# The end of a norm in front of the first product chain that needs it, in a two-layer diffusion trunk

## The chip, the cores and the metric

The kernel runs on one core of one Trainium2 chip. The metric is the device time of one execution in microseconds (us); less is better. The engines that matter here are TensorE (PE, matrix products into PSUM), VectorE (DVE), ScalarE (ACT), GpSimd (POOL) and the queue that starts the weight loads (SP).

## What is computed

Two layers of one trunk over 512 latent tokens and 256 context tokens, width 1024. Cut to what matters:

```python
for layer in range(2):
    h  = h  + 0.5*g1 *swiglu(prenorm(h,  norm_ffn1, sh1, sc1),  ffn1_w_in, ffn1_w_out)
    hc = hc + 0.5*cg1*swiglu(prenorm(hc, norm_ffn1, csh1, csc1), ffn1_w_in, ffn1_w_out)
    zl = prenorm(h, norm_mix, shm, scm) @ w_in      # even or odd mixer
    zc = prenorm(hc, norm_mix, cshm, cscm) @ w_in
    ...                                             # Fourier + GLA, or short conv + differential attention
    h = h + gm*(mix_l @ mix_w_out)
    h = h + 0.5*g2*swiglu(prenorm(h, norm_ffn2, sh2, sc2), ffn2_w_in, ffn2_w_out)
    ...                                             # hc likewise, but not in the last layer
return rmsnorm(h, final_norm)

def prenorm(h, gain, shift, scale):
    return h * rsqrt(mean(h*h) + 1e-6) * gain * (1 + scale) + shift
```

## The kernel before

Activations lie transposed: 8 blocks of 128 features, with tokens along the free dimension (latent 0 to 512, context 512 to 768). Every float32 product is three products of split operands, (hi,hi), (lo,hi) and (hi,lo); a weight tile of 128 x 1024 is loaded by the SP queue, ACT rounds it to its high half `wh` (L170) and DVE subtracts to get its low half `wl` (L171). In the odd mixer `wl_engine` is GpSimd, so there the low half is made by POOL. Four buffers hold split weights; a fifth split waits until the oldest of the four is used up.

A norm is *deferred*. The products run on h times gain and scale (`ah`, `al`, made by `scale`, L613 and L614), and the factor R = rsqrt(mean + eps) is multiplied in afterwards, when a product is taken out of PSUM (`scaled`, L315). R is made in these steps. `norm_acc` squares each finished block on ACT (L535, L540) and adds the squares up on POOL (L544), block by block while the output products of the stage before end. Then `rstd` sums over the partitions with a matmul by ones (two instructions on PE, as `n<-R,ones` or, in the odd mixer, `mm<-R,ones`), ACT makes Identity, Ln and Exp of it (L560, L561, L564), and DVE makes R with three steps (L565, L566, L568). Ahead of them `done` preloads ACT's table set for Ln and Exp (L575).

`out_phase` ends a stage. For the half of the tokens that it finishes first it calls `done` itself; for the second half it stores `pending = [LATE, half, norm]`, LATE = 3, and the next stage ends the norm: `project`, which makes one chain of 8 x 3 products of one weight tile and one half, counts down and calls `norm_late()` ahead of the fourth chain, or, if its own half overlaps the pending half, calls `norm_late(hf)` behind its chain. That happens five times, each time for the second half: (a) from the first feed-forward block into the even mixer at about 590 us of the span, (b) from the even mixer into the next feed-forward block at 930, (c) into the third one at 1465, (d) from it into the odd mixer at 2000, and (e) from the odd mixer into the last feed-forward block at 2335. In (a), (b), (c) and (e) the first four chains belong to the other half (or, in (e), the first 256 latent tokens), so the count ends the norm ahead of the fourth. In (d) `head_proj(0)` makes, for the key weights, one context chain and then one latent chain of 512 columns, whose half is the pending one: there the norm is ended behind the second chain. The query chains (two of 256) and the value chains (context, latent) follow.

The order of the work: instructions are traced in program order and numbered, and the framework then plans one queue per engine with times of its own: whenever an engine is free in that plan, it takes, of the instructions that the plan holds ready, the one with the lowest number. `high_priority(offset=n)` lowers the numbers of the instructions in its block by n. `keep_in_program_order` ties an instruction behind the one traced before it on its engine: the table preload of `done` is tied so, and so are, in a `weave` (`pin`), the matmuls. On the chip each queue runs in the planned order and waits where the chip is later than the plan. `self.both` is False in the two mixers until their last filler, and True in the feed-forward blocks. HIP is 300. In the odd mixer three PSUM buffers (`ps0`) take the chains of `project`: the fourth chain needs the first one's buffer, the fifth the second one's.

Of the kernel before, what the change touches and what calls it, by code (L numbers as in the profile page):

```python
# [37 lines left out]
HIP = 300  # L38
# [80 lines left out]
class Net:  # L119
# [150 lines left out]
    def project(self, which, w, m, hf, c):  # L270


        if self.pending:
            self.pending[0] -= 1
            if self.pending[0] < 0:
                self.norm_late()
        t0, t1 = hf
        n = t1 - t0
        ps = self.mmt(which)[:m]
        w = tuple(x[:, :, :m] for x in w) if m < P else w  # L280
        a0 = self.acol(t0)
        if not self.defer or c is not None:
            yield from self.chain(ps[:, :n], w, self.A, a0, a0 + n)
            self.norm_late(hf)
            return ps[:, :n], c
        before = a0 == self.scol + 2
        a0 = min(a0, self.scol)
        yield from self.chain(ps[:, :n + 2], w, self.A, a0, a0 + n + 2)
        self.norm_late(hf)
        c = self.cpool.tile([P, 2], F32, tag="c", name=self.nm("c"), bufs=6)[:m]  # L290
        o = 0 if before else n
        with self.evac():
            self.nc.vector.tensor_copy(c, ps[:, o:o + 2])
        return ps[:, 2 * before:2 * before + n], c

    def norm_late(self, hf=None):

        if self.pending:
            _, late, last = self.pending
            if hf is None or hf[0] < late[1] and late[0] < hf[1]:  # L300
                self.pending = None
                last.done(late)

    def evac(self):

# [997 lines left out]
    def odd_mixer(self, halves, last):  # L1303
# [12 lines left out]
        with ExitStack() as es:  # L1316
# [42 lines left out]
            def head_proj(h):  # L1359
# [9 lines left out]
                def project(w, jobs, dst, rot=None):  # L1369
                    c = None  # L1370
                    for hf in jobs:
# [12 lines left out]
                        yield 0  # L1384

                yield from project(ws[0], (CT, LT), kr, kr[:, 0:SEQ])
                T = p2.tile([P, 2, TOK], F32R, tag="T", name=self.nm("T"))
                for s, (own, oth) in enumerate(((lo, up), (up, lo))):
# [3 lines left out]
                    nc.gpsimd.dma_start(B(T[oth, s, :]), kr[own, :])  # L1392
                ws.append(self.load_w(ow[18 + h], KD))
                yield from project(ws[1], (L1, L0), qr, qr)
                Q = [None, None]

# [8 lines left out]
                while h and (h - 1, 1) not in scored:  # L1405
                    yield None
                stack(0)
                vt = p1.tile([P, TOK], F32, tag="vt", name=self.nm("vt"))
                yield from project(ws[2], (CT, LT), vt)
                v = (p2.tile([P, TOK], F32R, tag="vh", name=self.nm("vh")),  # L1410
                     p2.tile([P, TOK], F32R, tag="vl", name=self.nm("vl")))
# [347 lines left out]
```

## Time and profile before

| what | value |
|---|---|
| time, median of 3 runs | 2729.46 us (2728.81 to 2730.92) |
| profiled execution, time | 2728.34 us |
| profiled execution, span | 2726.5 us |
| PE busy | 2662.0 us, 98% of the span |
| DVE, ACT, POOL busy | 1965.1, 1114.2, 305.6 us |
| mean granted TensorE clock | 0.992 |

The span runs from the first to the last instruction; the time has 1.8 us around it. A busy PE is a pipeline with matmuls in it and not PE at its peak.

### The profile page before, as it was taken

The numbers are of one execution on the slowest core, as the hardware profiler recorded it, in microseconds if no ns is written. First come the engines' busy times: TensorE is split into PE (matmuls) and PEld (weight loads), VectorE is DVE, ScalarE is ACT, GpSimd is POOL, SyncE is SP. The second block draws the span as 40 slices with busy tenths as digits, with TensorE's granted clock in tenths as the row PEclk, the third lists the DMA queues.
The fourth block names the chain that finished last, engine by engine and source line by source line (L and its number), as shares of the span: only waits on it lengthen the run. The fifth ranks groups of instructions, "written<-read, shape, count | busy, mean of one in ns | idle before, by whom it ended". The sixth has DMA issues, their size and how long they took to land.

```text
span 2726.5 us, 42007 instructions
## 1 busy us (share of the span) xinstructions
PE 2662.0 (98%) x16718; PEld 2441.8 (90%) x16718; DVE 1965.1 (72%) x3415; ACT 1114.2 (41%) x1852; POOL 305.6 (11%) x313
## 2 busy tenths in 40 slices
PE   9999999999999999999999999999999999999998
PEld 6888888888888879999998899999978888999998
DVE  6699999777889876655666766656678887755545
ACT  4312121255545643323436534333456566523323
POOL 2000000030000200100002100000142323100002
PEclk9999999999999999999999999999999999999999
DMA  7466665622111034434422444334222222342332
GB/s 264 136 206 192 194 205 184 228 72 86 55 51 63 28 97 113 110 83 112 112 75 61 105 108 111 89 96 119 78 86 63 68 56 72 119 142 79 97 97 63
DMA packets 114276, 298.24 MB, mean 109 GB/s; under 512 B 13136, under 2 KB 22704, under 8 KB 114080
## 3 DMA queue, kind: packets, MB, share of 16 engines
q1 hardware_dynamic: 98448, 264.52, 30.4%
q0 software_dynamic: 14544, 29.99, 6.1%
q8 instruction: 132, 2.16, 0.3%
q10 hardware_dynamic: 1088, 1.05, 0.1%
q14 instruction: 64, 0.52, 0.1%
HBM read 285.55 MB, written 2.10 MB: 105 GB/s over the span
## 4 chain that ended last, share of the span: by engine, by line
PE 82%; DVE 12%; ACT 3%; issue 2%; DMA 1%; SPq 0%; POOL 0%; DVEq 0%; ACTq 0%; POOLq 0%
PE mm L176 80%; DVE al L614 1%; DVE hlat L639 1%; DVE mx L1444 1%; DVE gS L1245 1%; PE sc L176 1%; DVE wl L171 1%; ACT wh L170 1%; ACT e L1446 1%; PE n L176 1%; PE mm L183 0%; DVE atl L152 0%; DVE hctx L639 0%; DVE ry L1354 0%; DVE e L1458 0%
## 5 line engine op out<-in xcount | busy, mean ns | idle before, releaser
L176 PE MATMUL mm<-ah,wh 128*128 128x258 f32 (+3 forms) x2896 | 947.3, 327 | 7.5 <-DVE t L315 4.0
L176 PE MATMUL mm<-ah,wl 128*128 128x258 f32 (+3 forms) x2896 | 930.8, 322 | 3.4 <-DVE wl L171 3.4
L176 PE MATMUL mm<-al,wh 128*128 128x258 f32 (+3 forms) x2896 | 932.3, 322 | 0.0
L170 ACT ACTIVATE wh<-wr 128x1024 fp32r<-128x1024 f32 (+2 forms) x393 | 377.4, 960 | 798.4 <-PE mm L176 627.9
L176 PEld LDWEIGHTS mm<-ah,wh 128*128 128x128 f32 x2896 | 548.6, 189 | 43.5 <-DVE t L315 4.8
L176 PEld LDWEIGHTS mm<-ah,wl 128*128 128x128 f32 x2896 | 547.9, 189 | 34.6 <-DVE wl L171 5.0
L176 PEld LDWEIGHTS mm<-al,wh 128*128 128x128 f32 x2896 | 548.8, 190 | 27.5 <-issue 1.7
L176 PE MATMUL mm<-hh,wh 128*128 128x256 f32 (+1 forms) x1408 | 459.5, 328 | 9.2 <-DVE hctx L639 5.4
L176 PE MATMUL mm<-hh,wl 128*128 128x256 f32 (+1 forms) x1408 | 458.8, 327 | 2.1 <-DVE wl L171 2.1
L176 PE MATMUL mm<-hl,wh 128*128 128x256 f32 (+1 forms) x1408 | 459.4, 327 | 0.0
L171 DVE TENSOR_TENSOR wl<-wr,wh 128x1024 fp32r<-128x1024 f32 (+2 forms) x357 | 395.4, 1109 | 48.2 <-ACT wh L170 47.6
L176 PEld LDWEIGHTS mm<-hh,wh 128*128 128x128 f32 x1408 | 267.0, 190 | 38.0 <-DVE hctx L639 8.3
L176 PEld LDWEIGHTS mm<-hh,wl 128*128 128x128 f32 x1408 | 267.4, 190 | 26.6 <-DVE wl L171 2.7
L176 PEld LDWEIGHTS mm<-hl,wh 128*128 128x128 f32 x1408 | 267.6, 190 | 23.3
L639 DVE SCALAR_TENSOR_TENSOR hlat<-mm,mod,hlat 128x512 f32<-128x512 f32 (+1 forms) x248 | 163.1, 661 | 167.7 <-PE mm L176 167.1
L492 DVE SCALAR_TENSOR_TENSOR junk<-ada,cond 128x1024 bf16<-128x1024 f32 x224 | 273.0, 1219 | 3.4 <-DMA ada<-in_adaT_dram 3.0
L315 DVE TENSOR_TENSOR t<-mm,R 128x256 f32<-128x256 f32 (+1 forms) x216 | 106.5, 494 | 103.5 <-PE mm L176 103.0
L785 POOL DMA_DIRECT2D sg<-in_ffn_in_dram x80 | 71.0, 1015 | 849.5 <-DVE hctx L639 356.1
L151 ACT ACTIVATE hh<-t 128x256 fp32r<-128x256 f32 (+2 forms) x136 | 79.6, 585 | 174.2 <-DVE t L716 151.0
L544 POOL TENSOR_TENSOR nacc<-nacc,nsq 128x256 f32<-128x256 f32 x47 | 37.6, 800 | 969.8 <-ACT nsq L540 929.9
L858 DVE SCALAR_TENSOR_TENSOR t<-mm,R 128x386 f32<-128x386 f32 x40 | 22.4, 560 | 126.7 <-PE mm L176 126.7
L714 ACT ACTIVATE t<-t,c 128x256 f32<-128x256 f32 (+1 forms) x96 | 54.1, 563 | 136.5 <-DVE t L315 133.5
(317 smaller groups left out, 3657.7 us busy)
## 6 DMA issues: line engine op xcount, KB each, us to landing
wr<-in_ffn_in_dram SPq DMA_DIRECT2D x136, 512.0 KB, 3.4
ada<-in_adaT_dram SPq DMA_DIRECT2D x128, 512.0 KB, 3.8
wr<-in_ffn_out_dram SPq DMA_DIRECT2D x48, 512.0 KB, 4.1
sg<-in_ffn_in_dram SPq DMA_DIRECT2D x80, 256.0 KB, 3.1
sg<-in_ffn_in_dram POOLq DMA_DIRECT2D x80, 256.0 KB, 5.5
wr<-in_ffn_out_dram SPq DMA_DIRECT2D x48, 384.0 KB, 3.3
wr<-in_odd_w_dram SPq DMA_DIRECT2D x24, 512.0 KB, 3.3
wr<-in_even_w_dram SPq DMA_DIRECT2D x21, 512.0 KB, 3.3
```

What stands on the lines that cost most here:

```text
L151: self.nc.scalar.activation(hi, src, AF.Copy)
L170: self.nc.scalar.activation(hi, rv, AF.Copy)
L171: self.wl_engine.tensor_tensor(lo, rv, hi.bitcast(F32), op=ALU.subtract)
L176: i = self.nc.tensor.matmul(*a, **k)
L315: self.nc.vector.tensor_tensor(dst, ps, self.R[:ps.shape[0], hf[0]:hf[1]], op=ALU.mult)
L492: nc.vector.scalar_tensor_tensor(junk, w, 1.0, self.cond[:, s, :], op0=ALU.mult, op1=ALU.mult, accum_out=self.mods[l][:, s, n:n + 1]))
L544: self.acc_engine.tensor_tensor(acc[:, :w], acc[:, :w], sq[:, :w], op=ALU.add)
L614: nc.vector.scalar_tensor_tensor(lo[:, a], self.hv(k, s0, s1), G, hi[:, a].bitcast(F32), op0=ALU.mult, op1=ALU.subtract)
L639: nc.vector.scalar_tensor_tensor(hv, ps[:, s0 - t0:s1 - t0], gate, hv, op0=ALU.mult, op1=ALU.add)
L714: nc.scalar.activation(sg, sg, AF.Silu, bias=c[0][:, st:st + 1])
L785: nc.gpsimd.dma_start(out, y, accum_op=ALU.add)
L1245: nc.vector.scalar_tensor_tensor(S[r, c1, :], S[r, c0, :], EL[r, c0:c0 + 1], U[c0][r], op0=ALU.mult, op1=ALU.add)
```

## The change

Two edits. In `project`, where the count has not run out and `both` is False, a pending norm whose half overlaps the chain's own is ended in front of the chain and not behind it. And `norm_late` traces the end of the norm under a priority that is 300 numbers higher.

```diff
@@ -274,6 +274,8 @@
             self.pending[0] -= 1
             if self.pending[0] < 0:
                 self.norm_late()
+            elif not self.both:
+                self.norm_late(hf)
         t0, t1 = hf
         n = t1 - t0
         ps = self.mmt(which)[:m]
@@ -299,7 +301,8 @@
             _, late, last = self.pending
             if hf is None or hf[0] < late[1] and late[0] < hf[1]:
                 self.pending = None
-                last.done(late)
+                with self.tc.high_priority(offset=HIP):
+                    last.done(late)
```

## Rows read from the trace of the kernel before

**Rows 1.** Page, part 1: busy us (share of the span) xinstructions
```profile
PE 2662.0 (98%) x16718; PEld 2441.8 (90%) x16718; DVE 1965.1 (72%) x3415; ACT 1114.2 (41%) x1852; POOL 305.6 (11%) x313
```

**Rows 2.** Waits, PE: waiting for, us in total, times, longest
```profile
PE mm L176 <- DVE t L315: 4.0, 1, 4.0
```

**Rows 3.** Timeline, PE at (d): start, us, operation [idle before <- releaser]
```profile
1994.70 0.28 PE L176 MATMUL mm<-ah,wh 128*128 128x258 f32 x1
...
1997.60 0.39 PE L176 MATMUL mm<-ah,wh 128*128 128x512 f32 x1
...
2003.69 1.13 PE L176 MATMUL mm<-R,ones 128*128 128x512 f32 x2 [0.37 <-POOL R L544]
...
2010.25 0.28 PE L176 MATMUL mm<-ah,wl 128*128 128x256 f32 x1
2014.58 0.39 PE L176 MATMUL mm<-ah,wh 128*128 128x258 f32 x1 [4.04 <-DVE t L315]
```

**Rows 4.** Timeline, ACT at (d), behind the ones matmul
```profile
2006.48 0.51 ACT L1381 ACTIVATE kr<-kr,c 128x256 f32<-128x256 f32 x1 [4.86 <-DVE kr L315]
2007.00 1.28 ACT L575 ACT_TABLE_LOAD   x1
2008.30 1.06 ACT L170 ACTIVATE wh<-wr 128x1024 fp32r<-128x1024 f32 x1
2009.26 0.67 ACT L560 ACTIVATE R<-mm,eps 128x512 f32<-128x512 f32 x1
```

**Rows 5.** Timeline, DVE at (d)
```profile
2001.70 4.27 DVE L1348 SCALAR_TENSOR_TENSOR nlam<-lam 128x1 f32<-128x1 f32 x1
...
2011.20 1.14 DVE L565 TENSOR_TENSOR R<-R,t 128x512 f32<-128x512 f32 x1 [4.76 <-ACT t L564]
2012.38 0.69 DVE L566 SCALAR_TENSOR_TENSOR R<-R,t 128x512 f32<-128x512 f32 x1
...
2013.83 0.69 DVE L315 TENSOR_TENSOR t<-mm,R 128x512 f32<-128x512 f32 x1
```

**Rows 6.** Timeline, POOL at (d)
```profile
2002.35 1.29 POOL L544 TENSOR_TENSOR R<-R,nsq 128x512 f32<-128x512 f32 x1
2003.59 2.36 POOL L171 TENSOR_TENSOR wl<-wr,wh 128x1024 fp32r<-128x1024 f32 x1
2009.44 2.36 POOL L171 TENSOR_TENSOR wl<-wr,wh 128x1024 fp32r<-128x1024 f32 x1 [3.49 <-ACT wh L170]
```

**Rows 7.** Windows, PE alone: stretch, us, busy (instructions), granted clock, DMA
```profile
2015.04:2018.36 3.32, 3.32 (x18) 0.52 0.00 0
```

**Rows 8.** Timeline, ACT at (d), ahead of the ones matmul
```profile
1998.07 0.73 ACT L613 ACTIVATE ah<-hlat,mod 128x512 fp32r<-128x512 f32 x1 [2.84 <-DVE hlat L639]
...
1999.22 1.04 ACT L170 ACTIVATE wh<-wr 128x1024 fp32r<-128x1024 f32 x1
```

**Rows 9.** Timeline, PE and POOL at (b)
```profile
932.13 1.36 POOL L544 TENSOR_TENSOR R<-R,nsq 128x512 f32<-128x512 f32 x1 [0.74 <-ACT nsq L540]
935.57 6.72 POOL L544 TENSOR_TENSOR R<-R,nsq 128x512 f32<-128x512 f32 x3 [2.09 <-ACT nsq L540]
...
938.03 0.36 PE L176 MATMUL mm<-ah,wh 128*128 128x258 f32 x1 [0.71 <-DVE hlat L639]
...
943.95 1.02 PE L176 MATMUL n<-R,ones 128*128 128x512 f32 x2
```

**Rows 10.** Timeline, POOL and PE at (a)
```profile
597.58 1.30 POOL L544 TENSOR_TENSOR R<-R,nsq 128x512 f32<-128x512 f32 x1
...
602.40 1.02 PE L176 MATMUL n<-R,ones 128*128 128x512 f32 x2
```

**Rows 11.** Timeline, POOL at (c)
```profile
1468.57 1.32 POOL L544 TENSOR_TENSOR R<-R,nsq 128x512 f32<-128x512 f32 x1 [0.90 <-ACT nsq L540]
```

**Rows 12.** Timeline, POOL and PE at (e)
```profile
2332.95 3.28 POOL L544 TENSOR_TENSOR R<-R,nsq 128x256 f32<-128x256 f32 x3 [0.88 <-ACT nsq L540]
...
2335.69 0.39 PE L176 MATMUL mm<-ah,wl 128*128 128x258 f32 x1 [1.29 <-DVE wl L171]
```

## The prediction

> **What bounds the kernel now.** I read the page first, then the waits of PE, then the timelines of the four engines at the five places where a pending norm is ended. The page says that PE is busy for 98% of the span [rows 1]. So whatever this change does, it does by taking idle time of PE away or adding some. The waits of PE name one that belongs to a pending norm: a single wait of 4.0 us for the product that is multiplied by R [rows 2]. It lies at (d), the head of the odd mixer; at (a), (b), (c) and (e) no PE wait is put down to R.
>
> At (d) the reader is to see this. The context key chain starts at 1994.70, the latent one at 1997.60, the ones matmul follows it at 2003.69 after 0.37 us of waiting for POOL's last add, the query chains run until 2010.54, and the context chain of the values starts only at 2014.58, because the PSUM buffer of the latent key chain is not yet free [rows 3]. Behind the ones matmul ACT is held back: by an activation that comes after a late DVE step, then a table load of 1.28, then a weight split of 1.06 from 2008.30; only then comes the first step of R, at 2009.26 [rows 4]. DVE's three steps follow at 2011.20, the first of them slow at 1.14, and the product is read at 2013.83 [rows 5]. The wait has a second price: at 2015.04 to 2018.36 PE runs at a granted clock of 0.52, that is the lower of its two levels (1.2 GHz of 2.4 GHz), after it had stood idle for 4.04 us [rows 3, 7]. Sixteen product intervals lie in that stretch of 3.32 us. At the upper level one takes 0.121 (the 24 products of the context key chain fill 1994.70 to 1997.60 [rows 3]), so sixteen would take 1.94, and the stretch costs about 1.4 us.
>
> **The change, part by part.** Nothing is added or removed: the same two ones matmuls, three activations, one table load and three DVE steps are issued, no DMA is moved, and SP is passed by nothing. What changes is where they stand in four queues.
>
> First edit. It acts at (d) alone: in the even mixer the first four chains belong to the other half, so there the count still ends the norm, and the feed-forward blocks have `both` True. At (d) the ones matmul moves in front of the latent key chain in program order. The table load stays tied behind the same activation, since the chain that it is moved past has no ACT instruction.
>
> Second edit. All five ends get a number lower by 300. Three chains with their evacuations are some 100 numbers, so the ones matmul now beats all of the chains around it wherever the plan holds it ready, at all five places. That is the point on which I cost the change: PE's queue runs in order, and the ones matmul will stand where the *plan* expects POOL's last add, while the chip may be later. Queued behind it are the products of the running chain, which need nothing of R.
>
> How far is the plan ahead of the chip? At (d) the ACT queue tells it. The split at 1999.22 writes buffers that came free with the last output product, which on the chip came just ahead of 1994.70 [rows 3], and it stands behind the activation that the chip starts at 1998.07 after 2.84 us of idleness [rows 8]. Had the plan seen that idleness it would have filled it with the split; so in the plan that activation starts by 1994.7, at least 3.4 us ahead of the chip.
>
> At (d), then: R's last add ends on the chip at 2002.35 + 1.29 = 2003.64 [rows 6], and in the plan some 3.4 to 5 us earlier in the chip's reckoning, that is at 1998.6 to 2000.2, inside the latent key chain. PE will stop there until about 2003.7, for 3.5 to 5.1 us; I take the middle, 4.3. The bounds are today's 0.37 and 6.1 (a stop at the chain's very start, 2003.69 - 1997.60). After it PE has no reason to stop later: today's work ends at 2010.54 with 0.37 of waiting in it, so the value chain starts at 2010.54 - 0.37 + 4.3 = 2014.5 where it now starts at 2014.58. R's own path: ACT's split of 1.06 gives way [rows 4], and DVE's first step loses its stretch of 1.14 - 0.69 = 0.45 if POOL's half of that split no longer runs beside it [rows 5, 6], so the buffer is free 1.5 us earlier, at 2013.1, and no longer decides. The stall of 4.04 goes and one of 4.3 takes its place in front, with the same low clock behind it. Net: 0.0, between -1.5 -1.4 = -2.9 (no early stop, and the clock holds) and +1.7 (a stop of 6.1).
>
> At (b): the ones matmul stands at 943.95 today, but R is ready at 935.57 + 6.72 = 942.29 [rows 9]. The three adds take 6.72, while the one before took 1.36 and three of these 4.08: the chip may be 2.64 later than a plan in which nothing disturbs them, and the 0.71 that PE waits for the last block's update there is a second lateness of the same sort. Cost of a stop between 0 and 3.35; no row says which end, so I take the half, 1.7. PE has no later wait there that would swallow it.
>
> At (a) R is ready at 597.58 + 1.30 = 598.88, well ahead of today's ones matmul at 602.40 [rows 10]; (c) is of the same form, with its last add at 1468.57 [rows 11]. The adds are undisturbed, so the lateness should be no more than one of them: 0 to 1.3 each, and I take 0.65 each. At (e) R is ready at 2332.95 + 3.28 = 2336.23, and PE waits for a split until 2335.69 in any case [rows 12]: 0 to 0.54, taken as 0.3. Nothing is gained at these four: today R is there before the first latent evacuation asks for it or holds no one up, since no PE wait names it [rows 2].
>
> Precedence on ACT and DVE costs nothing: weight splits that give way by one or two steps have been made ahead of need everywhere but at (e), where PE already waits 1.29 for one [rows 12], and the norm's steps there come behind that split.
>
> Sum: 0.0 + 1.7 + 0.65 + 0.65 + 0.3 = +3.3. Against the profiled execution 2728.34 + 3.3 = 2731.6; the median of the runs shown is 1.1 above that execution, so the forecast is 2732.8 us.
>
> **A rule that speaks against the gain at (d).** While POOL's split half runs from 2003.59 for 2.36 us, a DVE step on one column per partition lasts from 2001.70 to 2005.97, and the first step of R lasts 1.14 where the next takes 0.69 while the next split half runs [rows 5, 6]. If the split gives way on ACT by the norm's three activations it starts at about 2010.1, and its POOL half at 2011.2, just on DVE's third step: that would hold until 2013.6, and the buffer would be free at about 2014.9, later than now. The Trainium skill, page "SBUF — State Buffer", section "SBUF: two separate sides", says of the port pair of VectorE and GpSimd that it is an exclusive lock, held for the whole instruction, and that the loser fully blocks. By that rule the trace agrees.
>
> **The rivals.** *It does what it says* (faster, but little): the plan is near the chip, so no queue stops early, and the wait at (d) shrinks by 1.5, from 4.04 to 2.5, with or without the low clock behind it: -1.5 to -2.9, middle -2.0, time 2727.5. For it speaks that today's ones matmul waits for POOL only 0.37 [rows 3]; against it the place of the split in ACT's queue [rows 8]. *The collision above*: no early stop, but DVE's third step held by POOL: +0.4, time 2729.9. *The stops are at their upper ends* (slower): if PE stops at (b) for 3.35, at (a) and (c) for 1.3, at (e) for 0.54 and at (d) for 6.1, that is 3.35 + 2.6 + 0.54 + 1.7 = 8.2, and a stop of over 3 us at (b) may bring the low clock's 1.4: +9.6, time 2739.1. It decides from the point where the plan puts POOL's last add ahead of the chip by more than 2 us at (b). *The whole wait at (d) goes*: 4.04 + 1.4 = 5.4, time 2724.1. Against it: the table load stays tied behind an activation that ends at 2007.0, so R cannot be there before about 2012.
>
> **How the numbers follow.** Forecast 0.48, it does what it says 0.25, collision 0.07, upper ends 0.15, whole wait 0.05. A measurement of this kernel tells about 0.2% from no change, 5.5 us: 2724.0 to 2734.9. Faster by more takes the whole wait or a reordering further on in the odd mixer: 0.06. Slower takes the upper ends and the upper part of the forecast, whose own range is 2729.5 to 2736: 0.21. The rest, 0.73, is within 0.2%. The range of 8 in 10 reaches from 2726.0 (the second case with nearly all of its 2.9) to 2737.5.
>
> **What would show it.** Right: the ones matmul at (d) stands inside the latent key chain with a PE wait of 3 to 5 us for POOL L544, and the wait for DVE t L315 is gone or under 1 us; at (b) the ones matmul stands ahead of 943 with a PE wait of 1 to 3 us for POOL L544; ACT's split follows the norm's activations at (d). Wrong: no PE wait names POOL L544 beyond today's, or the ones matmuls of (a), (b) and (c) stand where they stood; then the second case holds. A third step of DVE of 2 us at (d) would show the collision.

## The result, and the profile after

The changed kernel takes 2745.80 us (median of 6 runs, 2744.99 to 2746.51) against 2729.52 us (6 runs, 2728.81 to 2730.92): a ratio of 1.0059 with a 95% interval of 1.0046 to 1.0072, 16.3 us slower. The forecast was 2732.8 us, with a range that ended at 2737.5. The sign of the sum was right and its size a fifth of what came. The profiled execution takes 2744.99 us with a span of 2742.9.

Part 1 of the page shows that PE does the same work in a longer span [rows 1]: its busy time is 0.5 us longer, the span 16.4.

```profile
PE 2662.5 (97%) x16718; PEld 2440.6 (89%) x16718; DVE 1967.0 (72%) x3415; ACT 1113.8 (41%) x1851; POOL 305.5 (11%) x313
```

The waits of PE name what is new (waiting for, us in total, times, longest):

```profile
PE n L176 <- POOL R L547: 10.5, 4, 3.9
PE mm L176 <- DVE hctx L642: 6.9, 6, 1.5
PE mm L176 <- DVE hlat L642: 5.9, 9, 1.1
PE mm L176 <- POOL R L547: 5.4, 1, 5.4
PE mm L176 <- DVE wl L171: 4.2, 6, 1.2
PE sc L176 <- DMA Q<-Q: 2.0, 2, 1.5
```

Five waits for POOL's last add, 15.9 us in all, stand where the kernel before had one of 0.37 [rows 3]; the wait of 4.0 for `t` [rows 2] is gone. The waits for `hctx` and `hlat` (the hidden states after an update) grew by 1.5 and 1.0 (5.4 and 4.9 before), that for `wl` shrank by 1.4 (5.6 before), that for the query's transfer grew by 1.5 (0.5 before). The timeline of PE shows the five ends in order (start, us, operation, idle before and its releaser):

```profile
599.85 1.13 PE L176 MATMUL n<-R,ones 128*128 128x512 f32 x2 [2.29 <-POOL R L547]
...
945.81 2.07 PE L176 MATMUL n<-R,ones 128*128 128x512 f32 x2 [3.90 <-POOL R L547]
...
1480.24 1.12 PE L176 MATMUL n<-R,ones 128*128 128x512 f32 x2 [1.80 <-POOL R L547]
...
2016.87 2.07 PE L176 MATMUL mm<-R,ones 128*128 128x512 f32 x2 [5.43 <-POOL R L547]
...
2351.51 0.70 PE L176 MATMUL n<-R,ones 128*128 128x256 f32 x2 [2.50 <-POOL R L547]
```

At each end PE stands still at the ones matmul until R's last add is there: 2.29 at (a), 3.90 at (b), 1.80 at (c), 5.43 at (d), 2.50 at (e). At (b) and (d) the two instructions also last 2.07 us, where they took 1.02 and 1.13 before [rows 3, 9]: they run at the lower clock. The windows of PE alone show how long that holds (stretch, us, busy and instructions, granted clock, then DMA):

```profile
601.00:605.00 4.00, 4.00 (x35) 1.00 0.09 21
945.80:950.70 4.90, 4.89 (x17) 0.50 0.39 108
1482.00:1486.00 4.00, 4.00 (x35) 1.00 0.01 4
2016.80:2022.60 5.80, 5.74 (x12) 0.50 0.48 166
2353.00:2357.00 4.00, 4.00 (x36) 1.00 0.70 206
```

Behind the stops of (a), (c) and (e) the granted clock is 1.00; behind those of (b) and (d) it is 0.50 for 4.9 and 5.8 us, PE's level of 1.2 GHz. What this costs: at (b) the ones matmuls and 14 products run from 945.81 to 950.69, 4.88 us; at the upper level the ones take 0.56, the first product behind them 0.52 and thirteen more 0.121 each, 2.65; so 2.2. At (d) the ones and ten products of 512 columns take 5.98, from 2016.87 to 2022.85; at the upper level 0.56 + 0.64 + 9 x 0.231 = 3.28 (the 0.64 is the first such product behind the ones in the run call_wlv below); so 2.7.

Where the time came from, stage by stage: I take the starts of the ones matmuls of the *first* halves, which the change doesn't move, as marks, each named after the end that follows it (the table is worked out from their rows in the two timelines of PE).

| from mark to mark | before, us | after, us | difference |
|---|---|---|---|
| (a) to (b) | 338.35 | 340.90 | +2.55 |
| (b) to (c) | 533.17 | 539.99 | +6.82 |
| (c) to (d) | 529.52 | 532.42 | +2.90 |
| (d) to (e) | 341.19 | 343.19 | +2.00 |
| (e) to the last norm | 380.72 | 381.92 | +1.20 |

The start up to (a) is 0.95 longer; there the waits for the first weight transfers differ, and the mark lies between 579.1 and 581.6 in the kernels of this document, most of which leave that stretch as it was. The stops and the clock account for most of the rest: (a) 2.29; (b) 3.90 + 2.2, which leaves 0.7; (c) 1.80, which leaves 1.1; (d) 5.43 - 0.37 for POOL, less the 4.04 for `t`, less the 1.4 of low clock behind that [rows 3, 7], plus 2.7, which makes 2.3; at the first scores, where PE now waits 1.5 for the query's transfer and before 0.6 for `kr`, it is 2.8, and 2.0 at the next mark; (e) 2.50, less the wait of 1.29 for `wl` [rows 12], which the stop covers.

How far to trust the small remainders: in seven kernels that leave everything from (b) to (c) as it was that stretch takes 533.17 to 533.82 us, before being the shortest, so the 0.7 is hardly more than this scatter. In eight that leave (c) to (d) as it was it takes 529.52 to 529.89, so the 1.1 is more, and it came again in the run not_d; its cause is open. It is not the longer waits for `hctx` and `hlat`, 1.0 and 1.4 us more, 40 to 55 us behind the stops of (b) and (c): the run call_only has the same waits at (b), and hip25 at (c), without a stop there. The clock scatters too. From a ones matmul ahead of (e) (`mm<-osq,ones`, at 2293.88 before) to the mark of (e) the kernel before takes 27.59 us, with the granted clock at 0.50 for 6.7 us of them, the changed one 26.58 with 3.4, and head_late, a run below, 24.99 with none. So 1.0 came back there, and up to that matmul the changed kernel is 3.0 behind. The edits don't decide it: not_d and b_only both leave the odd mixer as it was and have 3.3 and 6.6 us of it.

At (d) ACT did what the change is for (timeline of ACT):

```profile
2019.63 0.51 ACT L1384 ACTIVATE kr<-kr,c 128x256 f32<-128x256 f32 x1 [4.79 <-DVE kr L318]
2020.14 1.28 ACT L578 ACT_TABLE_LOAD   x1
2021.43 0.69 ACT L563 ACTIVATE R<-mm,eps 128x512 f32<-128x512 f32 x1
2022.02 0.68 ACT L564 ACTIVATE t<-mm,eps 128x512 f32<-128x512 f32 x1
2022.73 0.63 ACT L567 ACTIVATE t<-t 128x512 f32<-128x512 f32 x1
2025.60 1.06 ACT L170 ACTIVATE wh<-wr 128x1024 fp32r<-128x1024 f32 x1 [2.24 <-PE mm L176]
```

The norm's three activations follow the table load at once, and the split comes 2.24 us behind them; before, it stood in front of them [rows 4]. R is no longer late, but PE had by then lost 5.43 us.

### The profile page after: what moved, and what is told of

It reads as the page before. It is cut to its first block, busy times and chain, and to the rows that moved or that the text cites. A ratio compares the mean times of both kernels' runs of the same rounds, so it can differ in the third digit from the quotient of the medians.

```text
span 2742.9 us, 42006 instructions
## 1 busy us (share of the span) xinstructions
PE 2662.5 (97%) x16718; PEld 2440.6 (89%) x16718; DVE 1967.0 (72%) x3415; ACT 1113.8 (41%) x1851; POOL 305.5 (11%) x313
```

## The experiments

Two theories to begin with. *The plan's lead*: each end's ones matmul now stands in PE's queue where the plan holds R ready; the chip is later, and PE stops for the difference. *Precedence*: splits that give way on ACT and DVE, or the moved call, make the loss. A first answer is in the plans: a variant that raises the ones matmul alone, and leaves ACT's and DVE's steps their numbers, is planned into the same five queues as the whole change; one that raises only those steps, at the old calls, is planned into before's queues, with at most one table load of ACT in another place. So in the plan the priority acts through the ones matmul. By the places in PE's queue it stands 49, 47, 49 and 51 instructions ahead of its old place at (a), (b), (c) and (e), and 22 at (d).

**One edit alone** (call_only). The first edit without the priority:

```diff
-                with self.tc.high_priority(offset=HIP):
-                    last.done(late)
+                last.done(late)
```

> The first edit alone: the norm's end in front of the chain, no priority. On PE only the ones matmul of (d) moves, by 22 places, into the latent key chain as with the whole change; those of (a), (b), (c) and (e) stand as before. Theory 1 (the loss is made at each end where the ones matmul stands ahead of POOL's last add, and is the stop there plus the low clock behind it): only (d) pays, +2.0 us, 2731.5 us, with one PE wait of about 5.4 us for POOL at (d) and none at the other ends. Rival (the moved call makes the loss): about 2745 us. Rival (the change gains at (d)): below 2729 us.

It measured 2730.93 us, ratio 1.0006 (0.9997 to 1.0015), 1.3 us more. PE's timeline at (d):

```profile
2004.32 2.07 PE L176 MATMUL mm<-R,ones 128*128 128x512 f32 x2 [5.43 <-POOL R L546]
```

The stop is the one of the whole change, with no other wait for POOL; the marks give +1.57 from (d) to (e). The time's interval includes no difference; that the stop is there, and that nothing moved elsewhere, is read from the rows.

**The other four places alone** (not_d). The priority at (a), (b), (c) and (e), (d) as before:

```diff
-            elif not self.both:
-                self.norm_late(hf)
...
+                self.ends += 1
-                with self.tc.high_priority(offset=HIP):
+                with self.tc.high_priority(offset=HIP if self.ends in (1, 2, 3, 5) else 0):
```

> The priority at (a), (b), (c) and (e), with (d) ended behind the latent key chain and without priority, as before. Theory 1: the whole change less the 2.0 us of (d): +14.3, 2743.8 us, four PE waits for POOL as with the whole change, and the wait of 4.0 us for t at (d) is back. Rival (the odd mixer's head makes the loss): about 2731 us.

It measured 2742.77 us, ratio 1.0048 (1.0035 to 1.006), +13.2. The waits of PE:

```profile
PE n L177 <- POOL R L547: 10.5, 4, 3.9
PE mm L177 <- DVE t L318: 4.0, 1, 4.0
```

The four stops and the old wait at (d) are there as expected. This run and the one before add up to +14.5 of the 16.3. In its profile the clock also fell behind the stop of (a), where it had held in the whole change; the last section comes back to that.

**One place alone** (b_only). The same for (b) alone:

```diff
-                with self.tc.high_priority(offset=HIP if self.ends in (1, 2, 3, 5) else 0):
+                with self.tc.high_priority(offset=HIP if self.ends in (2,) else 0):
```

> The priority at (b) alone, without the first edit. Theory 1: a stop of 3.9 us for POOL at (b), the clock at 0.50 for some 5 us behind it (2.2 us), and 0.5 to 1 us more at the next stage's start: +6.1 to +7.1, 2735.7 to 2736.7 us, and nothing at the other ends. Rival (the stop alone costs, the clock is hidden): +3.9, 2733.5 us.

It measured 2736.64 us, ratio 1.0027 (1.0016 to 1.0037), +6.5: the stop and the clock behind it.

```profile
942.98 2.07 PE L177 MATMUL n<-R,ones 128*128 128x512 f32 x2 [3.91 <-POOL R L547]
...
944.00:949.00 5.00, 5.00 (x25) 0.58 0.21 59
949.00:955.00 6.00, 6.00 (x52) 1.00 0.00 0
```

The first line is of the timeline, the others are windows as above: granted clock 0.58 in the first 5 us, 1.00 behind. By the marks (b) to (c) is 6.98 longer, so the rival, the stop of 3.9 alone, falls.

**The dose** (hip35 and hip25). The whole change with 35 and with 25 in place of 300. The ones matmul of (b) then stands 17 and 24 products later than with 300.

```diff
-                with self.tc.high_priority(offset=HIP):
+                with self.tc.high_priority(offset=35):
```

> The whole change with an offset of 35 numbers in place of 300. The ones matmuls of (a), (b), (c), (e) then stand 30 products ahead of their old place and not 47 to 51, so 19, 17, 19 and 21 products later than with 300; (d) as with 300. Theory 1: a product is 0.121 us, so the stops shrink by 2.3, 2.1, 2.3 and 2.5 us: from 2.29, 3.90, 1.80 and 2.50 to 0, 1.8, 0 and 0, and after a stop of 1.8 us the clock stays at 1.00. Sum 1.8 to 2.8 at (b) and 2.0 at (d): 2733.3 to 2734.3 us. Rival (precedence over the splits on ACT and DVE makes the loss; any priority does it): about 2745 us.

> The whole change with an offset of 25. The ones matmul of (b) stands 7 products later than with 35 and 24 later than with 300. Theory 1: a stop of 1.0 us for POOL at (b) (1.88 less 7 x 0.121), none at (a), (c) and (e), 5.4 at (d): +1.0 and, if the clock falls behind it as in hip35, +1.6 at (b), +1.5 at (d): 2732 to 2733.5 us. Rival (the stop at (b) doesn't follow the place in the queue): 1.9 us or more there, 2733.5 us or more.

They measured 2733.44 us (1.0013, 1.0005 to 1.0022) and 2732.91 us (1.0011, 1.0002 to 1.002). PE at (b), with 35 and then with 25:

```profile
938.44 0.36 PE L176 MATMUL mm<-ah,wh 128*128 128x258 f32 x1 [0.71 <-DVE hlat L642]
942.72 1.18 PE L176 MATMUL n<-R,ones 128*128 128x512 f32 x2 [1.88 <-POOL R L547]
```

```profile
940.55 0.36 PE L176 MATMUL mm<-ah,wh 128*128 128x258 f32 x1 [0.74 <-DVE hlat L642]
944.84 1.12 PE L176 MATMUL n<-R,ones 128*128 128x512 f32 x2 [1.03 <-POOL R L547]
```

Stops of 3.90, 1.88 and 1.03 at places 17 and 7 products apart: 2.02 and 0.85, or 0.119 and 0.121 a product. The stop follows the place in the queue product by product; the waits of PE name no stop at (a), (c) and (e) in either. One step of the expectation failed: with 35 the clock fell behind a stop of 1.88. The windows show it, first for 35 and then, where it held, for 25:

```profile
944.00:945.00 1.00, 1.00 (x7) 0.50 0.00 1
...
946.00:947.00 1.00, 1.00 (x7) 0.50 0.55 192
947.00:948.00 1.00, 1.00 (x10) 0.96 0.00 0
```

```profile
945.00:947.00 2.00, 2.00 (x12) 1.00 0.35 112
```

So (b) cost 3.49 with 35 by the marks and 0.97 with 25. The rival of the first of the two expectations falls: any priority gives the norm's steps precedence, and with 35 the time is 2733.4 and not about 2745.

**What makes the plan early at (d)** (call_wlv). The first edit alone, the first head's low halves on DVE:

```diff
+            self.wl_engine = nc.vector
             self.run(head_proj(0))
+            self.wl_engine = nc.gpsimd
```

> The first edit alone, with the low halves of the first head's weights made by DVE and not by POOL. Theory 1a (the plan is ahead of the chip at (d) because POOL's split halves hold DVE steps, 2.64 us for one of 0.75, and the adds, 1.76 for 1.29, which the plan does not have): the stop for POOL at (d) falls by about 2.4 us, from 5.4 to about 3; the time by 2.4 us or, if the clock holds, by up to 5.2: 2725.7 to 2728.5 us. Rival 1b (the lead comes from something else): a stop of 5 us or more, 2730 to 2732 us.

It measured 2727.70 us, ratio 0.9994 (0.9984 to 1.0003), by the ratios 0.0012 of the time, 3.3 us, under the first edit alone; each interval is 0.0009 wide to either side, so it is the rows that show the gain. PE at (d), and DVE's third step of R beside POOL:

```profile
2000.42 1.12 PE L176 MATMUL mm<-R,ones 128*128 128x512 f32 x2 [1.71 <-POOL R L546]
2016.09 0.47 PE L176 MATMUL mm<-ah,wh 128*128 128x512 f32 x1 [0.82 <-DVE t L317]
```

```profile
2007.72 0.69 DVE L568 SCALAR_TENSOR_TENSOR R<-R,t 128x512 f32<-128x512 f32 x1
2008.44 2.77 DVE L570 SCALAR_TENSOR_TENSOR R<-R,t 128x512 f32<-128x512 f32 x1
```

```profile
2007.98 2.68 POOL L171 TENSOR_TENSOR wl<-wr,wh 128x1024 fp32r<-128x1024 f32 x1 [5.29 <-ACT wh L170]
```

The stop falls from 5.43 to 1.71 at the same place in PE's queue, more than the 2.4 expected, and the clock holds. Part of the gain comes back ahead of the first scores, where PE waits 3.4 for the query's transfer (1.4 in the first edit alone). So 3.7 of the 5.4 us went with POOL's split halves; that the plan leaves out how these hold DVE's steps is my reading of it, and no run shows the plan's own times. Nor does a run tell this from a plainer way: the halves stand in POOL's own queue too, just ahead of adds (in the changed kernel a half runs from 2007.64 for 2.41 us and the next add starts at 2010.00, as it ends). The 1.7 left, and the leads of (a), (b), (c) and (e), where the splits are DVE's own, were not taken apart. R's last add also stands behind three DMA issues in POOL's queue (it starts at 1999.09, its square was done at 1998.27), but the plan seems to count such issues: in head_late_call below one of the three comes behind the add, and both the add and the place of the ones matmul move forward, by 0.5 us and by two products of 0.23. The third step of R, 2.77 us beside POOL's split half of 2.68, is the collision of the prediction's second rival; it happens here, and not in the changed kernel.

**Is R held at (d) by the place of the ones matmul?** (lam_late) The kernel before with the lambda block (one DMA, two DVE sums, an Exp, `nlam`) moved behind the first head's projection:

```diff
-            lv = self.tmp.tile([P, self.tmpw], F32, tag="t", name=self.nm("lv"))[:, :256]
-            nc.gpsimd.dma_start(lv, a["lam"].to_broadcast([P, 256]))
...
-            nc.vector.scalar_tensor_tensor(nlam, lam[:, 1:2], -LAM_INIT, lam[:, 0:1], op0=ALU.add, op1=ALU.subtract)
...
             self.run(head_proj(0))
+            lv = self.tmp.tile([P, self.tmpw], F32, tag="t", name=self.nm("lv"))[:, :256]
...
```

> The kernel before, with the small lambda steps (one DMA, two DVE sums, one Exp, nlam) traced behind the first head's projection and not ahead of it. Theory: at (d) it is not the ones matmul's place that holds R back but ACT, which waits 4.86 us for a context key product that stands on DVE behind the nlam step of 4.27 us; without that step the norm's first activation starts some 3 to 4 us earlier, PE's wait of 4.04 us falls under 1 us and the low clock of 1.4 us behind it goes: -4.0 to -5.4, 2724 to 2725.5 us. Rival (R is held by POOL's last add or by the table load): the wait stays at 3 us or more, 2728 to 2730 us.

It measured 2727.21 us, ratio 0.9992 (0.9983 to 1.0001), an interval that just includes no difference. DVE and PE at (d):

```profile
2005.38 0.15 DVE L1336 TENSOR_SCALAR dn<-dn 128x1 f32<-128x1 f32 x1 [1.68 <-DMA dn<-in_diff_norm_dram]
2005.54 0.43 DVE L315 TENSOR_TENSOR kr<-mm,R 128x256 f32<-128x256 f32 x1
```

```profile
2014.19 0.39 PE L176 MATMUL mm<-ah,wh 128*128 128x258 f32 x1 [1.79 <-DVE t L315]
```

The wait for `t` falls from 4.04 to 1.79 and the clock behind it stays at 1.00, so the step of 4.27 [rows 5] was in R's way. But not as much as expected: behind it the product `kr` stands for the `dn` step, and that for its DMA. In front of the first scores the query's transfer is now waited for 2.1 us, and there the kernel is 2.3 us ahead of the one before. By the marks the whole stretch from (d) to (e) is 3.3 us shorter; the last 1.0 came ahead of (e), where the clock is low for 3.4 us and not 6.7.

**The rest of the constants moved too** (head_late), to the same place:

```diff
-            cw = cp.tile([P, 2, 4], F32, name="cw")
-            nc.gpsimd.dma_start(cw, a["conv"])
-            dn = cp.tile([P, 1], F32, name="dn")
-            nc.gpsimd.dma_start(dn, a["diff_norm"])
-            nc.vector.tensor_scalar(dn, dn, 1.0 - LAM_INIT, None, op0=ALU.mult)
```

> The kernel before, with all the small constants of the odd mixer (lambda, the dn step and the two DMAs of cw and dn) traced behind the first head's projection. In lam_late the context key product on DVE still stood 1.68 us behind the dn step, which waited for its DMA; that goes. Theory (R at (d) is held by ACT, and ACT by that product): the norm's first activation comes 1.7 us earlier than in lam_late, PE's wait for t falls from 1.8 to 0 to 0.3 us: 2727.2 - 1.6 = 2725.6 us (2725 to 2726.5). Rival (the wait left is that of the table load and the split): no further gain, 2727 us.

It measured 2725.69 us, ratio 0.9988 (0.9979 to 0.9997): the time came as expected, for another reason. The wait for `t` is still 1.79:

```profile
2005.79 0.43 DVE L315 TENSOR_TENSOR kr<-mm,R 128x256 f32<-128x256 f32 x1 [1.34 <-POOL R L544]
```

```profile
PE mm L176 <- DVE t L315: 1.8, 1, 1.8
PE sc L176 <- DMA Q<-Q: 0.6, 1, 0.6
```

`kr` now waits 1.34 for POOL's last add, though the context part of R that it reads is older. The wait stands in the program, in the kernel before too: `kr` reads columns 512 to 768 of R and the add writes 0 to 512, but its semaphore is set to POOL's count behind that last add, as if R were one value. So the activation of `kr` on ACT, and the table load and the norm's activations behind it, wait for that add as well. The wait of PE that shrank is the one for the query's transfer, 0.6 in place of lam_late's 2.6; at the first scores the kernel is 2.8 us ahead of the one before. By the marks (d) to (e) is 5.1 shorter; 2.6 of them came in the last stretch ahead of (e), where the granted clock is 1.00 throughout.

**The first edit on top of that** (head_late_call):

```diff
+            elif not self.both:
+                self.norm_late(hf)
```

> head_late with the first edit added. The ones matmul of (d) stands two products further ahead than with the change. Theory 1 (PE stops for what the plan is ahead of the chip; nothing behind it is left to win): a stop of about 5.4 us and a low clock of 2.8 us behind it, with no later wait that they replace: about 8 us over head_late, 2733.5 us (2732 to 2735). Rival (the edit gains once the way on ACT is free): 2725.5 us or less.

It measured 2733.82 us, ratio 1.0016 (1.0007 to 1.0026), 8.1 us over head_late on the same chip.

```profile
2004.80 2.07 PE L176 MATMUL mm<-R,ones 128*128 128x512 f32 x2 [5.36 <-POOL R L546]
```

Nothing is left for the edit to win; its stop and the clock (0.50 from 2004 to 2009) are all there.

**Both obstacles out, without the change** (head_late_wlv): head_late with the first head's low halves on DVE.

```diff
+            self.wl_engine = nc.vector
             self.run(head_proj(0))
+            self.wl_engine = nc.gpsimd
```

> head_late with the low halves of the first head's weights made by DVE (as in call_wlv). In head_late the context key product waits on DVE for POOL's last add (1.34 us), so it is POOL that holds ACT and with it R. Theory: the adds come 3 us earlier, the product and the norm's activations 1.4 us, PE's wait for t falls from 1.8 to 0.4; part of that comes back in the wait for the query transfers ahead of the first scores: 2724.5 us (2724 to 2725.7). Rival (POOL's next split half falls on DVE's third step of R, as in call_wlv where it took 2.77 us): the wait stays at 1.8 or more, 2726 us or more.

It measured 2724.36 us (2723.35 to 2725.60), ratio 0.9978 (0.9969 to 0.9987): faster than both kernels.

```profile
2001.98 0.43 DVE L315 TENSOR_TENSOR kr<-mm,R 128x256 f32<-128x256 f32 x1 [1.32 <-POOL R L544]
2008.71 1.03 DVE L565 TENSOR_TENSOR R<-R,t 128x512 f32<-128x512 f32 x1 [4.39 <-ACT t L564]
2011.22 0.69 DVE L315 TENSOR_TENSOR t<-mm,R 128x512 f32<-128x512 f32 x1
```

```profile
PE sc L176 <- DMA Q<-Q: 2.6, 2, 2.0
```

`kr` is made at 2001.98, R's first step starts at 2008.71, `t` ends at 2011.91, and PE has no wait for `t` nor for POOL at (d). What is late next is the query's transfer again, 2.6 us. Up to the ones matmul ahead of (e) this kernel is 4.8 us ahead of the one before, and 1.0 more came by the clock in the last stretch.

## Why the prediction was wrong

**What held.** The mechanism: priority puts the ones matmul where the plan has R, PE's queue runs in order, and a stop appears at all five ends. The signs named ahead appeared: at (d) the ones matmul inside the latent key chain, the wait for `t` gone, the split behind the norm's activations, at (b) a stop for POOL. That nothing is gained at the other four held too, and nothing in the runs puts a loss down to precedence on ACT and DVE.

**The terms that were too small.** All five, by the size of the lead.

| end | forecast (bounds) | stop measured | stage measured |
|---|---|---|---|
| (a) | 0.65 (0 to 1.3) | 2.29 | +2.55 |
| (b) | 1.7 (0 to 3.35) | 3.90 | +6.8 |
| (c) | 0.65 (0 to 1.3) | 1.80 | +2.9 |
| (d) | 0.0 net, stop 4.3 (3.5 to 5.1) | 5.43 | +2.0 |
| (e) | 0.3 (0 to 0.54) | 2.50 | +1.2 |

The step that failed is "the adds are undisturbed, so the lateness should be no more than one of them". It bounds the lead by the disturbance of the last steps alone, at 1.3 us; the stops at (a) and (c) measured 2.29 and 1.80. That the plan is ahead by all that piles up on the way to R is my reading. At (a) the last add is not undisturbed either: it starts at 598.52, though ACT had its square done at 597.70, behind two DMA issues and a memset in POOL's queue (timeline of POOL, the changed kernel):

```profile
598.02 0.41 POOL L1015 MEMSET t<- 2x384 f32 x1
598.52 1.28 POOL L547 TENSOR_TENSOR R<-R,nsq 128x512 f32<-128x512 f32 x1
```

Whether the plan counts these 0.8 us no run at (a) shows; at (c) the add follows its square within 0.15 us. What makes the leads of (a) and (c) stays open. At (b) I saw two signs, 2.64 and 0.71 [rows 9], and took the half of their sum, 3.35, which as a whole was near the 3.90. At (e) I let the ones matmul stand no earlier than the product that waits for a split [rows 12]; it stood ahead of that, and only because the stop covers that wait does the stage cost half of its stop. (d) was read best, from a queue order that shows where the plan had an activation [rows 8]; that reading exists for (d) alone.

**The terms that were missing.** The low clock behind the stop at (b), 2.2 us, was in a rival and not in the forecast; at (d) I let the new low clock cost what the old one had, 1.4, and it cost 2.7, since it fell on products of 512 columns and held for 5.8 us. And some 1.1 us behind the stop of (c) were in no part of the sum; what they are is open.

**The rivals.** "The stops are at their upper ends" was the case that came, with its mechanism and its place, and its price of +9.6 was too low by the same bounds and by the clock, of which it has 1.4 at (b) alone. "It does what it says" falls with the five rows of waits. "The collision" is real but lies elsewhere. "The whole wait goes" came true without the change, with the obstacles moved (head_late_wlv): the objection that the table load stays tied behind a late activation was right, and that activation was the thing to free. "No DMA is moved" was not quite so: on POOL the two transfers of `T` are issued ahead of a split half now and behind it before, and ACT has one table load less [rows 1]; no wait of PE names them.

**The rule that was set beside the trace.** The Trainium skill, page "SBUF — State Buffer", section "SBUF: two separate sides", has a GpSimd instruction and a VectorE one of certain kinds, with two inputs in SBUF among them, lock each other out of their port pair for a whole instruction. The runs agree where they show it directly: R's third step, which has two such inputs and takes 0.69 elsewhere, took 2.77 beside a half of 2.68. I weighed it for one late step, and not for the lead, 3.7 of whose 5.4 us at (d) went with POOL's split halves; how much of that is the lock and how much POOL's own queue no run shows.

## What to carry to other kernels

A priority moves an instruction to where the *plan* has its input, and on an engine that never idles an in-order queue then pays the whole lead of the plan over the chip, here 1.8 to 5.4 us at each place, plus a lower clock at two of them. Find out first which step really holds the late value: here it was a context product on DVE behind a step on one column, and POOL's split halves beside it; moving those gained 5.6 us (4.8 by the rows of PE, without the part of the clock ahead of (e)), while raising the five ones matmuls lost 16. Dose the priority before you use it: some 30 products of lead in place of 50 took three of the five stops away.

## What the runs showed of the chip that was not expected

The length of a stop doesn't say whether the clock falls. Behind the stop of 2.29 us at (a) the granted clock held at 1.00 in the whole change; behind the same stop in not_d it fell, and (a) to (b) took 4.08 us more than before and not 2.55:

```profile
599.25 1.12 PE L177 MATMUL n<-R,ones 128*128 128x512 f32 x2 [2.29 <-POOL R L547]
...
600.50:603.80 3.30, 3.30 (x17) 0.50 0.09 23
```

Behind the wait of 1.79 for `t` it held in lam_late (first line) and fell in head_late (second line):

```profile
2014.00:2018.00 4.00, 3.81 (x28) 1.00 0.02 9
...
2014.80:2018.20 3.40, 3.40 (x19) 0.50 0.00 0
```

So the fall behind 1.88 in hip35 and the hold behind 1.03 in hip25 don't show a bound, nor that the short wait of 0.71 ahead of the first had a part in it. A forecast can give such a stop the price of the clock with a chance, not as a yes or no.

A DVE step on one column per partition, started just ahead of a row of POOL steps, ended with them, 4.27 us later in the kernel before and 4.26 in call_wlv [rows 5, 6].
